# mLSTM decay rows loaded a step ahead, gate columns and sample squares moved, latent-stage weights in tiles of their own

## The chip, the cores and the metric

The kernel runs on one core of a Trainium2 chip. A core has TensorE (PE: matrix products and transposes; its weight loads are shown as PEld), VectorE (DVE), ScalarE (ACT), GpSimd (POOL) and SyncE (SP). Each engine works off its own instructions in order. A DMA is started by an instruction in the queue of SP, ACT or POOL, and then runs beside the engines. The metric is the time of one execution in device microseconds, and the median of several executions is compared.

## The reference

One inference step of a two-layer decoder trunk with a width of 1024. It works on 1024 new tokens of one sequence (the prompt) and on one new token for each of 8 running sequences (the samples), all in float32. The samples carry an mLSTM state in the first layer and 8192 cached positions, in pages of 128, in the second.

```python
# layer 0: x += mlstm(rmsnorm(x)); x += swiglu(rmsnorm(x))
q, k, v, o, gates = split(x @ w_in)         # 8 heads, 64 wide for q and k, 128 for v
i_pre = gates[:8];  log_f = log_sigmoid(gates[8:])
# chunk by chunk, per head; b is the running sum of log_f, m_t a running maximum
w_inter = exp(b + m - m_t)
w_intra = exp(b_t - b_s + i_s - m_t)        # for s <= t
s   = (q k^T) * w_intra
num = w_inter * (q C) + s v
den = w_inter * (q n) + sum(s)
h   = num / max(|den|, exp(-m_t))
C   = w_C * C + (w_s k)^T v;  n = w_C * n + sum(w_s k)
out = (rmsnorm_per_head(h) * g_head * sigmoid(o)) @ w_out

# layer 1: x += mla(rmsnorm(x)); x += swiglu(rmsnorm(x)); final rmsnorm
cq, ckv, k_rope = split(x @ w_in)           # 384, 256, 64 columns
q = rmsnorm(cq) @ w_uq                      # 8 heads, 128 plain + 64 rotary columns each
k_nope, v = rmsnorm(ckv) @ w_uk, rmsnorm(ckv) @ w_uv
out = softmax(q k^T * scale, causal) v @ w_o    # samples: over the cached pages as well
```

The outputs are the new activations, the new mLSTM states and the new latent and rotary key rows.

## The kernel before

**Products.** A product of two float32 matrices is made of three products in a faster format, since each factor is split in a high and a low part: `mm3` (L133 to L136) issues high x high, high x low and low x high into one PSUM bank. `split` makes the parts: ACT rounds a tensor to its high part (L117, or L120 with a scale per row), DVE or POOL subtracts it from the tensor for the low part (L118, L121). Activations lie transposed, features on the 128 partitions and tokens along the free axis, in chunks of 344 columns (1024 prompt and 8 sample tokens). A weight tile has 1024 rows and 128 columns. `load_w` loads one on SP's queue into one of two "wr" buffers and splits it into one of two pairs of "wh" and "wl" buffers; `linear` takes its products with all token chunks and hands each bank to an evacuation function.

**Order.** The order on each engine is not written out by hand. A scheduler of the tile framework places the instructions when the kernel is built, with the order of the program as priority, a cost model of its own, and the buffers: a tile asked for beyond its count of `bufs` waits until an older one of the same tag is released. Moving a call in the program therefore moves it in the priorities of all engines.

**mLSTM.** After the normalised input, the q and k tiles, the gates and the eight v tiles are computed (`mlstm`). `narrow` (L444) projects the 16 gate columns. `gates` (L534 to L590) turns them into running sums and maxima on 8 partitions and writes two sets of rows to memory: G_d, from which the decay between two tokens follows, and wi_d, the weights of the old state. It ends with eight transposes (L589), two groups of four, copied into `tok` (L590), which holds the per-token columns: a_t, w_s and exp(-m_t).

The loop at L485 then runs 16 steps, step i for chunk i//2 of 128 tokens and for half i%2 of the heads. A step is `mlstm_chunk`. It asks for Gb, a DMA of four rows of G_d spread over all 128 partitions (L600), and wb, two DMAs of rows of wi_d (L601 to L604), all on ACT's queue. From Gb, a_t and the causal mask DVE makes the exponent (L609, once per head), ACT its exponential (L610), and DVE multiplies it with the scores (L617). kt is k transposed and weighted by w_s (L623), vn is v transposed (L629) with a column of ones, qw is q times wb, on POOL (L634). PE forms the outputs from vn with Gb and from the state with qw (L642, L644), and the state's increment (L654); DVE updates the state C (L660), with the last column of wb as its factor; dn, the normalisation and its reciprocal square root follow on DVE (L202, L203 and L668 to L680). The step stops there (`yield`) and is finished a step later: the normalised output is transposed back and copied into v (L683, L684).

Between the first part of a step and the end of the step before stands other work of PE. For steps 1 to 8 it is `proj_o(i - 1)`, one tile of the output gate: its banks are read by DVE (L462) into `ot`, put through a tanh by ACT (L463) and stored to o_d. For steps 9 to 14 it is a tile of the output projection. `mlstm_sample` (L686 to L800) is a generator for the samples' states: it is advanced by one a step, twice in step 3, up to step 8. Each piece loads the state of one sequence (s_C), updates it on DVE (L781) and takes its products; the last piece takes the remaining products, s_h and its squares, and on PE the sum of the squares over the partitions (L796). In step 8 the input's buffers are released, o_d is loaded back (L473) and the first half of the tokens is gated (L478).

**Latent stage.** `mla` (from L1265) projects the kv latents (two tiles, `ev_k`), the 64 rotary key columns (`narrow`, `ev_r`) and three tiles of query latents (`ev_q`). The weights w_uk and w_uv, as two halves each, are needed later in split form in memory (uw_d). `up(i, f)` (L1339 to L1351) does one half: it loads it into a "wr" buffer on SP, for w_uk also transposes it, splits it into the pair "wh" and "wl" and stores both on POOL's queue. up(0, 0) and up(0, 1) follow the first two query tiles, up(1, 0) and up(1, 1) the third (L1353 to L1360).

`queries` (from L1425) makes each head's query. wq (L1432 to L1434) holds all of w_uq, three loads of 768 KB on POOL's queue. `rotary(0)` (L1455) and `plain(0)` (L1486) load their own columns of the first heads; the other heads split theirs out of wq. Queries are stored to qn_d and qr_d, and attention loads them back, for the first head on ACT's queue (L1585, L1587).

**Attention.** It mixes the prompt's heads with units of the samples' pages. The change touches four small DVE operations on one value per partition: the sum of two partial sums (L1679, 32 of them), the running maximum (L1829, 16), the running sum (L1836, 16) and its final scaling (L1863, 8). In the page loop DVE transposes the gathered rows (L1815) for PE (L1822).

The rest of the kernel, both feed-forward layers among it, is not touched.

## Time and profile before

| | us |
|---|---|
| median of 3 executions | 2671.79 |
| lowest and highest | 2664.44 and 2671.98 |
| the profiled execution | 2671.14 |
| span of the profiled execution | 2669.1 |
| gates and v tiles, about | 117 to 232 |
| the 16 mLSTM steps, about | 232 to 475 |
| output projection and first feed-forward layer, about | 475 to 1215 |
| latent projections, about | 1216 to 1305 |
| latent queries, about | 1305 to 1380 |
| attention, about | 1380 to 1885 |
| output projection, second feed-forward layer, end | 1885 to 2669 |

The profile shows one execution. The span runs from its first to its last instruction, and the rest of the time lies around it. Times of a row are us from the start of the span. In a row of the timeline stand the start, the duration, the engine, the line in the kernel, the operation, the tile written and the tiles read, their shapes, how many instructions of the kind stand in a row, and in brackets how long the engine had been idle before and what ended that. A tile's name is that of the program, but `wh`, `zh`, `ss`, `sc` and `mm` are used at many places. An idle engine costs time only if it is on the path that sets the end.

### The profile page before, as it was taken

Reading aid. Unit: us, or ns where it says so; the run is one execution under the profiler, and the core shown is the slowest. Engines: PE = TensorE matmul, PEld = TensorE weight load, DVE = VectorE, ACT = ScalarE, POOL = GpSimd, SP = SyncE. Lnnn points to the kernel's source line nnn. Section 1 sums busy time; section 2 is a strip of 40 time slices with the busy share of each in tenths; the row PEclk is TensorE's granted clock in tenths of the full one; section 3 lists DMA queues with packets and bytes.
Section 4 is the critical chain, followed back from the end, with each engine's and each line's share of the span. In section 5 each row is a group of like instructions: output and inputs, shape, how many; then the busy total and the mean of one; then the engine's idle time right before and its main releaser. Section 6 shows DMA issues by size and latency. Waiting matters only on the chain.

```text
span 2669.1 us, 54244 instructions
## 1 busy us (share of the span) xinstructions
PE 2523.4 (95%) x21151; PEld 2382.9 (89%) x21151; DVE 1865.6 (70%) x4491; ACT 1326.3 (50%) x3281; POOL 571.0 (21%) x574
## 2 busy tenths in 40 slices
PE   8999988999999999999888888889999999999998
PEld 8998886999999999999876666667899999999998
DVE  4345668898777777566557786667498877777755
ACT  4122234556555666453344555546355666555543
POOL 1000102201111111122334445442220111111102
PEclk9999989999999999999888999989999999999999
DMA  5133446526666656553666676554634756665653
GB/s 191 40 71 84 127 130 137 157 72 132 129 125 131 118 116 131 116 161 106 223 225 231 230 251 218 203 202 167 201 104 100 139 112 124 127 134 117 121 126 115
DMA packets 342519, 383.36 MB, mean 144 GB/s; under 512 B 23434, under 2 KB 274703, under 8 KB 333943
## 3 DMA queue, kind: packets, MB, share of 16 engines
q0 software_dynamic: 58880, 181.24, 29.2%
q1 hardware_dynamic: 258982, 182.30, 22.8%
q10 hardware_dynamic: 24400, 16.36, 2.6%
q8 instruction: 166, 2.72, 0.4%
q14 instruction: 91, 0.74, 0.1%
HBM read 254.12 MB, written 125.70 MB: 142 GB/s over the span
## 4 chain that ended last, share of the span: by engine, by line
PE 70%; DVE 13%; DMA 8%; ACT 4%; issue 3%; POOL 1%; SPq 1%; another core or an unknown queue 0%; POOLq 0%; ACTq 0%; DVEq 0%
PE sc L134 13%; PE sc L136 13%; PE sc L135 13%; PE mm L134 5%; PE mm L136 5%; PE mm L135 5%; DVE tt L1815 3%; PE ss L1847 2%; PE ss L134 2%; PE ss L136 2%; PE ss L135 2%; DMA Gb<-G_d 2%; PE ss L1822 2%; DVE wl L118 1%; PE mm L1718 1%
## 5 line engine op out<-in xcount | busy, mean ns | idle before, releaser
L1159 POOL DMA_DIRECT2D x_d<-wl x72 | 86.8, 1205 | 1003.1 <-DVE wl L1158 348.8
L117 ACT ACTIVATE wh<-wr 128x512 fp32r<-128x512 f32 (+2 forms) x169 | 136.6, 809 | 193.4 <-PE mm L135 125.1
L1815 DVE STREAM_TRANSPOSE tt<-nat 128x1024 f32<-128x1024 f32 x128 | 154.1, 1223 | 10.7 <-PE ss L1822 6.7
L118 DVE TENSOR_TENSOR wl<-wr,wh 128x1024 fp32r<-128x1024 f32 (+2 forms) x82 | 98.4, 1200 | 37.2 <-ACT wh L117 28.5
L134 PE MATMUL mm<-zh,wh 128*128 128x344 f32 x320 | 104.7, 327 | 8.0 <-DVE ot L462 8.0
L1822 PE MATMUL ss<-tt,qbd 128*32 128x128 f32 x2560 | 94.6, 283 | 16.1 <-DVE tt L1815 10.8
L118 DVE TENSOR_TENSOR b<-u,b 128x256 fp32r<-128x256 f32 (+1 forms) x252 | 103.2, 423 | 9.2 <-ACT b L117 7.9
L117 ACT ACTIVATE b<-u 128x256 fp32r<-128x256 f32 (+1 forms) x252 | 98.8, 414 | 15.8 <-PE ss L136 6.3
L1159 POOL DMA_DIRECT2D x_d<-st x72 | 105.1, 1459 | 4.2 <-DVE dC L118 4.2
L118 DVE TENSOR_TENSOR wh<-S,wh 128x512 fp32r<-128x512 f32 x108 | 74.6, 690 | 42.5 <-ACT wh L117 42.5
L135 PE MATMUL mm<-zl,wh 128*128 128x344 f32 x320 | 103.8, 324 | 0.0
L136 PE MATMUL mm<-zh,wl 128*128 128x344 f32 x320 | 103.6, 324 | 0.0
L1822 PEld LDWEIGHTS ss<-tt,qbd 128*32 128x32 f32 x2560 | 73.0, 113 | 33.7 <-DVE tt L1815 20.1
L117 ACT ACTIVATE wh<-S 128x512 fp32r<-128x512 f32 x108 | 67.9, 629 | 59.5 <-PE sc L136 39.8
L1718 PE MATMUL mm<-wh,vt 128*128 128x256 f32 (+1 forms) x320 | 76.7, 301 | 10.6 <-ACT wh L117 5.5
L134 PE MATMUL sc<-zh,wh 128*128 128x344 f32 x256 | 83.0, 325 | 1.0 <-ACT wh L117 0.8
L136 PE MATMUL sc<-zh,wl 128*128 128x344 f32 x256 | 82.1, 321 | 0.7 <-DVE wl L118 0.7
L135 PE MATMUL sc<-zl,wh 128*128 128x344 f32 x256 | 82.1, 321 | 0.0
L1718 PEld LDWEIGHTS mm<-wh,vt 128*128 128x128 f32 x320 | 56.9, 199 | 22.0 <-ACT wh L117 9.2
L1677 ACT ACTIVATE wr<-sc,mx,rqt 128x512 f32<-128x512 f32 (+2 forms) x96 | 64.1, 673 | 20.7 <-DVE mx L1672 10.8
L1808 POOL DMA_INDIRECT nrp<-in_cache_k_rope_dram,idx x64 | 61.8, 966 | 56.3 <-DVE tt L1815 21.7
L1807 POOL DMA_INDIRECT nat<-in_cache_latent_dram,idx x64 | 61.1, 954 | 57.2 <-PE ss L1847 43.6
(1075 smaller groups left out, 10678.0 us busy)
## 6 DMA issues: line engine op xcount, KB each, us to landing
wr<-in_ffn_w_gate_up_dram SPq DMA_DIRECT2D x96, 512.0 KB
x_d<-st POOLq DMA_DIRECT2D x72, 520.0 KB
x_d<-wl POOLq DMA_DIRECT2D x72, 512.0 KB
dr<-in_ffn_w_down_dram SPq DMA_DIRECT2D x72, 256.0 KB
wr<-in_mlstm_w_in_dram SPq DMA_DIRECT2D x24, 512.0 KB
wr<-in_mlstm_w_out_dram SPq DMA_DIRECT2D x16, 512.0 KB
q<-qn_d SPq DMA_DIRECT2D x28, 256.0 KB
wr<-in_mla_w_o_dram SPq DMA_DIRECT2D x14, 512.0 KB
```

The costliest lines, as they stand in the source:

```text
L117: ins = nc.scalar.activation(hi, src, AF.Copy)
L118: self.low = e.tensor_tensor(lo, src, hi.bitcast(F32), op=ALU.subtract)
L134: mm(ps, wh, xh, start=start, stop=False, **kw)
L135: mm(ps, wh, xl, start=False, stop=False, **kw)
L136: self.last = mm(ps, wl, xh, start=False, stop=stop, **kw)
L1159: nc.gpsimd.dma_start(self.x_d[:, 2 * dp:2 * dp + 2, 512 * i:512 * i + 2 * PW[i]], st[i], accum_op=ALU.add)
L1677: nc.scalar.activation(px[:, ks], o, AF.Exp, bias=mx[:, 0:1], scale=f, accum_out=sm[:, c:c + 1])
L1718: nc.tensor.matmul(o, x, y, start=i == 0, stop=i == len(ops) - 1)
L1807: nc.gpsimd.indirect_dma_start(out=nat[:, s].rearrange("p s c -> p (s c)"), out_offset=None, in_=lat, in_offset=ix)
L1808: nc.gpsimd.indirect_dma_start(out=nrp[:, s].rearrange("p s c -> p (s c)"), out_offset=None, in_=rop, in_offset=ix)
L1815: V.transpose(out=tt, in_=src.rearrange("p s (c i) -> p c s i", i=32))
L1822: nc.tensor.matmul(psS[32 * j:32 * j + 32, u * P:u * P + P], self.qbd[:, b, cb], tt[:, c, 4 * j:4 * j + 4].rearrange("p s k -> p (s k)"), ...
```

## The change

Six edits. (1) `gates` no longer makes the transposes into `tok`; it returns them as a function, `turned`, which is called after the fifth v tile. (2) The loads of Gb and wb move out of `mlstm_chunk` into `decay`. The loop calls it for the first step ahead of the loop and then in each step for the next one. Gb has four buffers instead of three, wb three as before, qw one instead of two. The factor of the state update, which was read from wb, is copied to a small tile wc by POOL first. (3) The sample generator has one more `yield`, ahead of the sum of squares, and step 8 advances it once more, ahead of the last output-gate tile. (4) `up` writes its parts to tiles uh and ul of a pool of its own. up(1, 0) stands after the second kv tile and up(1, 1) after the rotary key columns. (5) wq holds five heads (3 to 7), 480 KB a load; the plain columns of heads 1 and 2 come by two loads on ACT's queue into a "wr" tile, `pair`; four tiles of the rotary step are asked for ahead of wq. (6) The four small operations of attention become tensor-scalar forms, in which a per-partition operand takes the place of one or two of the tensors.

```diff
@@ mlstm
-        self.gates(p1, pg, gi, lf, bcol)
+        turned = self.gates(p1, pg, gi, lf, bcol)
...
         for j in range(8):
             proj_v(j)
+            if j == 4:
+                turned()
...
+        due = [self.decay(pi, 0, 0)]
         for i in range(16):
-            g = self.mlstm_chunk(pi, i // 2, i % 2, q, k, v)
+            if i < 15:
+                due.append(self.decay(pi, (i + 1) // 2, (i + 1) % 2))
+            g = self.mlstm_chunk(pi, i // 2, i % 2, q, k, v, *due.pop(0))
             next(g)
+            if i == 8:
+                next(smp, None)
             if 1 <= i <= 8:
                 proj_o(i - 1)
...
@@ gates
-        for hf in range(2):
-            ps = self.tp()
-            ...
+        def turned():
+            for hf in range(2):
+                ps = self.tp()
+                for j in range(4):
+                    c = hf * 4 + j
+                    nc.tensor.transpose(ps[:, j * 96:(j + 1) * 96], p3[:, c * L:(c + 1) * L], self.ident[:96, :96])
+                V.tensor_copy(self.tok[:, hf * 4:hf * 4 + 4], ps[:, :384].rearrange("p (j i r) -> p j i r", j=4, i=3)[:, :, :, 0:8])
+        return turned
...
+    def decay(self, pi, c, hg):
+        nc = self.nc
+        s = slice(c * L, (c + 1) * L)
+        Gb = self.t(pi, [P, 4, L], "Gb", bufs=4)
+        nc.scalar.dma_start(Gb, self.G_d[hg * 4:hg * 4 + 4, s].unsqueeze(0).to_broadcast([P, 4, L]))
+        wb = self.t(pi, [P, 2, L], "wb", bufs=3)
+        for hh in range(2):
+            src = self.wi_d.rearrange("(hp hh) s -> hh hp s", hh=2)[hh, hg * 2:hg * 2 + 2, s]
+            nc.scalar.dma_start(wb[hh * 64:(hh + 1) * 64], src.unsqueeze(0).to_broadcast([64, 2, L]))
+        return Gb, wb
...
@@ mlstm_chunk
-            qw = self.t(pi, [P, 2, L], "qw", bufs=2)
+            qw = self.t(pi, [P, 2, L], "qw", bufs=1)
             nc.gpsimd.tensor_tensor(qw, q[:, j2, s], wb, op=ALU.mult)
+            wc = self.t(pi, [P, 2], "wc", bufs=3)
+            nc.gpsimd.tensor_copy(wc, wb[:, :, L - 1])
...
-                V.scalar_tensor_tensor(C[r, h], C[r, h], wb[r, h // 2, L - 1:L], ps[r, h // 2], op0=ALU.mult, op1=ALU.add)
+                V.scalar_tensor_tensor(C[r, h], C[r, h], wc[r, h // 2:h // 2 + 1], ps[r, h // 2], op0=ALU.mult, op1=ALU.add)
@@ mlstm_sample
         V.tensor_tensor(h2, hs, hs, op=ALU.mult)
+        yield
         ps = self.tp()
         nc.tensor.matmul(ps[:, 0:64], self.ones, h2, start=True, stop=True)
@@ mla
+        upp = self.pool("up")
...
-            wh, wl = (self.t(self.wp, [P, KT * P], x, F32R) for x in ("wh", "wl"))
+            wh, wl = (self.t(upp, [P, KT * P], x, F32R) for x in ("uh", "ul"))
...
         self.linear(lw(QL + P, P), z, KT, P, ev_k(1))
+        up(1, 0)
         self.page_index(mt)
...
         self.narrow(wr, 64, 64, z, "wh", ev_r)
+        up(1, 1)
...
-        for f in range(2):
-            up(1, f)
@@ queries
+        self.rf = [[self.t(qs, [P, CW], "rf" + i, bufs=2) for i in "ab"] for _ in range(2)]
-        wq = self.t(qs, [P, 3, 8, 192], "wq")
+        wq = self.t(qs, [P, 3, 5, 192], "wq")
         for k in range(3):
-            nc.gpsimd.dma_start(wq[:, k].rearrange("p h c -> p (h c)"), wuq[k * P:(k + 1) * P, :])
+            nc.gpsimd.dma_start(wq[:, k].rearrange("p h c -> p (h c)"), wuq[k * P:(k + 1) * P, 576:])
...
-            raw = wq[:, :, h, 0:P]
             if h == 0:
...
+                pair = self.t(self.wp, [P, KT * P], "wr")[:, : 6 * P].rearrange("p (k h m) -> p k h m", h=2, m=P)
+                for i in range(2):
+                    nc.scalar.dma_start(pair[:, :, i], self.wsrc(wuq, 0, 3, 192 * (i + 1), P))
+                first.append(pair)
+            else:
+                raw = first[0][:, :, h - 1] if h < 3 else wq[:, :, h - 3, 0:P]
@@ attention
-                    V.tensor_tensor(sm[:, 0:1], sm[:, 0:1], sm[:, 1:2], op=ALU.add)
+                    V.tensor_scalar(sm[:, 0:1], sm[:, 0:1], sm[:, 1:2], None, op0=ALU.add)
...
-        V.scalar_tensor_tensor(nb, rm, -SCALE, self.nb, op0=ALU.mult, op1=ALU.min)
+        V.tensor_scalar(nb, rm, -SCALE, self.nb, op0=ALU.mult, op1=ALU.min)
...
-        V.scalar_tensor_tensor(self.lrow, self.lrow, al, ls, op0=ALU.mult, op1=ALU.add)
+        V.tensor_scalar(self.lrow, self.lrow, al, ls, op0=ALU.mult, op1=ALU.add)
...
-            V.tensor_tensor(self.lrow, self.lrow, fac, op=ALU.mult)
+            V.tensor_scalar(self.lrow, self.lrow, fac, None, op0=ALU.mult)
```

More of the change, by code (lines that the diff above doesn't have):

```diff
@@ L513, in mlstm @@
                     gated(*loaded(ob()[:, :256], 1, h, first))
-        tiles = [self.t(pi, [P, 4, L], "Gb", bufs=3).rearrange("p h t -> p (h t)")] + [ob() for _ in range(3)]
+        tiles = [self.t(pi, [P, 4, L], "Gb", bufs=4).rearrange("p h t -> p (h t)")] + [ob() for _ in range(3)]
         tiles += [self.t(pi, [P, 4, 129], "vn", bufs=3).rearrange("p h t -> p (h t)") for _ in range(2)] + [ob() for _ in range(2)]
@@ L584, in gates, with mlstm_chunk @@
         self.tok = self.t(p1, [P, NCK, 3, 8], "tok")
-        for hf in range(2):
-            ps = self.tp()
-            for j in range(4):
-                c = hf * 4 + j
-                nc.tensor.transpose(ps[:, j * 96:(j + 1) * 96], p3[:, c * L:(c + 1) * L], self.ident[:96, :96])
-            V.tensor_copy(self.tok[:, hf * 4:hf * 4 + 4], ps[:, :384].rearrange("p (j i r) -> p j i r", j=4, i=3)[:, :, :, 0:8])
-    def mlstm_chunk(self, pi, c, hg, q, k, v):
+        def turned():
[16 more added lines that the diff above has]
+        return Gb, wb
+    def mlstm_chunk(self, pi, c, hg, q, k, v, Gb, wb):
         nc = self.nc
@@ L598, in mlstm_chunk @@
         j2 = slice(hg * 2, hg * 2 + 2)
-        Gb = self.t(pi, [P, 4, L], "Gb", bufs=3)
-        nc.scalar.dma_start(Gb, self.G_d[h4, s].unsqueeze(0).to_broadcast([P, 4, L]))
-        wb = self.t(pi, [P, 2, L], "wb", bufs=3)
-        for hh in range(2):
-            src = self.wi_d.rearrange("(hp hh) s -> hh hp s", hh=2)[hh, j2, s]
-            nc.scalar.dma_start(wb[hh * 64:(hh + 1) * 64], src.unsqueeze(0).to_broadcast([64, 2, L]))
         a_t, ws_t, em_t = (self.tok[:, c, r, h4] for r in range(3))
@@ L1351, in up @@
                 nc.gpsimd.dma_start(self.uw_d[i, k, :, f], x.bitcast(F32))
+        lw = lambda c0, m: self.load_w(self.wsrc(w_in, 0, KT, c0, m), KT, m)
+        for a in self.lead:
+            ev_k(0)(*a)
+        self.linear(lw(QL + P, P), z, KT, P, ev_k(1))
+        up(1, 0)
+        self.page_index(mt)
+        wr = self.t(self.wp, [P, KT * P], "wr")[:, :KT * 64].rearrange("p (k m) -> p k m", m=64)
+        nc.sync.dma_start(wr, self.wsrc(w_in, 0, KT, QL + KVL, 64))
+        self.narrow(wr, 64, 64, z, "wh", ev_r)
+        up(1, 1)
+        self.rs_of(s2, KVL)
+        for c in range(NCH):
+            cs = slice(c * CW, (c + 1) * CW)
+            w = slice(c * CW, min((c + 1) * CW, S))
+            for j in range(2):
+                V.scalar_tensor_tensor(kf[:, j, cs], kf[:, j, cs], self.gcol(self.G_KV + j), s2[:, cs], op0=ALU.mult, op1=ALU.mult)
+                self.split(ckh[:, j, w], ckl[:, j, w], kf[:, j, w], lo_eng=nc.gpsimd)
         for j in range(3):
@@ L1398, in mla @@
         mt.release()
+        upp.release()
         self.rsp.release()
@@ L1455, in rotary @@
         def rotary(h0):
-            raw = wq[:, :, h0:h0 + 4, P:]
+            raw = wq[:, :, 1:, P:]
             if h0 == 0:
@@ L1473, in chunk @@
                 for e, (x, y) in enumerate(((rc, rn), (rn, rc))):
-                    f, g = (self.t(qs, [P, CW], "rf" + i, bufs=2) for i in "ab")
+                    f, g = self.rf.pop(0) if self.rf else (self.t(qs, [P, CW], "rf" + i, bufs=2) for i in "ab")
                     V.tensor_tensor(f, ps[0], x[:, cs], op=ALU.mult)
@@ L1502, in plain @@
             return chunk
-        stores = []
+        stores, first = [], []
         for op in ORDER.split():
```

15 lines of the change are left out of this document (removed).

## The prediction

> **What bounds the kernel now.** I read the page first, then busy times by stage, then the waits of TensorE (PE) and VectorE (DVE) in the stages that the change touches, and last the timelines around each wait. The page's span, busy line and chain of waits:
>
> ```profile
> span 2669.1 us, 54244 instructions
> ...
> PE 2523.4 (95%) x21151; PEld 2382.9 (89%) x21151; DVE 1865.6 (70%) x4491; ACT 1326.3 (50%) x3281; POOL 571.0 (21%) x574
> ...
> PE 70%; DVE 13%; DMA 8%; ACT 4%; issue 3%; POOL 1%; SPq 1%; another core or an unknown queue 0%; POOLq 0%; ACTq 0%; DVEq 0%
> ```
>
> PE is busy 95% of the span, and 70% of the chain is PE. No matrix product goes away in this change, so the most that can be won is PE's idle time, 2669.1 - 2523.4 = 145.7 us, and PE's time at a low clock, and only where the change acts. By stage (window, length, busy time of PE, PEld, DVE, ACT, POOL, PE's granted clock, DMA share, GB/s): mLSTM steps with the output gate, the later steps, latent projections (two rows), latent queries, the middle of attention.
>
> ```profile
> 245.00:410.00 165.00, 150.40 (x993) 138.66 (x994) 106.44 (x343) 54.53 (x159) 15.37 (x25) 0.93 0.48 135
> 410.00:475.00 65.00, 56.27 (x340) 44.88 (x339) 55.05 (x191) 27.64 (x86) 16.86 (x19) 0.97 0.54 109
> 1215.00:1256.00 41.00, 39.53 (x259) 37.01 (x257) 26.93 (x67) 13.72 (x27) 4.70 (x6) 1.00 0.22 78
> 1256.00:1305.00 49.00, 46.57 (x294) 43.84 (x293) 24.48 (x48) 22.42 (x43) 25.04 (x32) 0.93 0.52 166
> 1305.00:1380.00 75.00, 68.38 (x404) 64.30 (x402) 47.28 (x137) 32.70 (x75) 17.26 (x27) 0.89 0.66 232
> 1500.00:1700.00 200.00, 170.92 (x2183) 136.37 (x2187) 148.06 (x319) 106.90 (x280) 98.79 (x97) 0.99 0.68 231
> ```
>
> PE idles 14.6, 8.7, 1.5, 2.4, 6.6 and 29.1 us in these. All of what follows fits inside these numbers, the gates' 4.55 us and the clocks of 0.89 and 0.93.
>
> **Gate columns (turned).** PE, in order, came to the eight transposes of L589 before their rows were ready:
>
> ```profile
> 152.83 0.88 PE L589 MATMUL ss<-ct,p 96*128 96x96 f32 x8 [3.04 <-ACT p L577]
> ...
> 172.78 0.63 ACT L610 ACTIVATE Gb<-Gb 128x512 f32<-128x512 f32 x1 [6.62 <-DVE Gb L609]
> ...
> 174.41 0.43 PE L134 MATMUL sc<-zh,wh 128*128 128x344 f32 x1 [0.83 <-ACT wh L117]
> 175.67 0.42 PE L136 MATMUL sc<-zh,wl 128*128 128x344 f32 x1 [0.68 <-DVE wl L118]
> ```
>
> The 0.88 us of transposes are the same work wherever they stand. Placed after the fifth v tile, they wait for rows that were complete some 30 us before, and v products stand where the 3.04 us wait was. The second group has the same cure by another way: ScalarE (ACT) stood 6.62 us at L610, an exponential of the first step's decay that had been drawn forward into the v products, and the v weights' split L117 was queued behind it. The decay needs tok, and tok now comes later, so L610 cannot stand there. 3.04 + 0.83 + 0.68 = 4.55 us; I take 4, since the v tile that moves up may be short of its own weights by a fraction. Ends 1 and 4.55.
>
> **Decay rows a step ahead.** Waits (engine, line, cause: us in all, times, longest): DVE at 245 to 475, DVE at 410 to 475, and PE at 117 to 460.
>
> ```profile
> DVE Gb L609 <- DMA Gb<-G_d: 27.5, 9, 5.4
> DVE s_C L781 <- DMA s_C<-in_state_mlstm_C_dram: 10.1, 5, 6.0
> ...
> DVE Gb L609 <- DMA Gb<-G_d: 5.2, 3, 2.3
> ...
> PE mm L134 <- DVE ot L462: 8.0, 6, 2.4
> PE ss L796 <- DVE s_h L794: 1.2, 1, 1.2
> PE ss L654 <- DVE sfu L202: 2.4, 1, 2.4
> ```
>
> DVE's 27.5 us are not the price: an idle DVE costs only where PE comes to wait. How it does is seen in one step, and a second one looks alike but is not:
>
> ```profile
> 310.06 1.14 DVE L609 SCALAR_TENSOR_TENSOR Gb<-Gb,tok,ct 128x128 f32<-128x128 f32 x4 [4.05 <-DMA Gb<-G_d]
> 314.77 0.52 DVE L462 TENSOR_TENSOR ot<-mm,rs 128x344 f32<-128x344 f32 x1
> 315.35 0.55 PE L134 MATMUL mm<-zh,wh 128*128 128x344 f32 x1 [2.36 <-DVE ot L462]
> ...
> 290.71 0.69 DVE L781 TENSOR_TENSOR s_C<-s_C,s_wsb 128x512 f32<-128x512 f32 x1 [6.04 <-DMA s_C<-in_state_mlstm_C_dram]
> 296.01 0.42 PE L134 MATMUL mm<-zh,wh 128*128 128x344 f32 x1 [2.30 <-DVE ot L462]
> ```
>
> DVE waits for the decay rows, its queue holds the eviction L462 of an output-gate product, and PE waits for that bank. At 296 the late one is the sample state's load s_C, which the change does not touch. So 8.0 - 2.30 = 5.7 us hang on Gb. With four buffers and the load traced one step ahead, a step of about 20 us (eight in the 165 us above) lies between issue and use. s_C then becomes the late one, in the steps where it is late already. I take 4 of 5.7 (ends 0 and 5.7) and 1 us for the clock, which is 0.93 over this stage (ends 0 and 2).
>
> After 410 us DVE is busy 55.05 of 65 us: it sets the pace, so its 5.2 us of Gb waits could count in full, but behind them stand its other partners (PE, ACT). I take 2, ends 0 and 5.2.
>
> Issues: the three triggers a step are those of before, on the same ACT queue, so no issue time is added; the first step's three are joined by the second's before the loop, where ACT is idle over half of the time. The new copy wc is 14 POOL instructions, at most 0.73 us by the nearest larger one,
>
> ```profile
> 268.02 0.73 POOL L634 TENSOR_TENSOR qw<-q,wb 128x256 f32<-128x256 f32 x1 [15.02 <-PE sc L644]
> ```
>
> and POOL is busy 15.4 of 165 us here; the state update L660 that reads wc waits for PE's L654 anyway. Nothing; uncovered, 14 x 0.73 = 10 us of POOL. One qw buffer instead of two is paid by the same 15.02 us of POOL's idle time.
>
> **Sample squares.** In the ninth step PE waits 1.2 us at L796 for s_h. With the split it goes on with gate products. But the output of that step then waits for its o_d reload, and the 2.4 us at L654 sit behind the gating that this feeds, so what is won early is partly waited for there. I take 0.5, ends 0 and 1.2.
>
> **Latent projections and queries.** PE's waits at 1215 to 1380, then the rows at the places:
>
> ```profile
> PE sc L134 <- ACT wh L117: 7.1, 3, 4.0
> PE sc L136 <- DVE wl L118: 1.6, 4, 0.7
> ...
> 1216.33 0.63 ACT L117 ACTIVATE wh<-wr 128x512 fp32r<-128x512 f32 x1 [8.23 <-PE mm L135]
> 1245.00:1255.00 10.00, 8.55 (x53) 8.11 (x51) 9.81 (x22) 4.47 (x9) 0.57 (x1) 1.00 0.10 39
> 1252.72 1.06 ACT L117 ACTIVATE wh<-wr 128x1024 fp32r<-128x1024 f32 x1 [1.06 <-DVE wl L118]
> 1317.77 0.42 PE L134 MATMUL sc<-cqh,wh 128*128 128x344 f32 x1 [3.99 <-ACT wh L117]
> 1317.19 0.94 ACT L117 ACTIVATE wh<-wq 128x384 fp32r<-128x384 f32 x2 [3.67 <-DMA qr_d<-qx]
> 1316.64 0.37 ACTq L1585 DMA_DIRECT2D q<-qn_d  x1
> 1315.00:1325.00 10.00, 6.50 (x25) 6.06 (x26) 5.50 (x20) 2.59 (x6) 2.16 (x4) 0.70 0.77 256
> 1325.00:1335.00 10.00, 10.00 (x63) 10.00 (x62) 5.17 (x13) 5.08 (x12) 0.00 (x0) 0.96 0.71 253
> ```
>
> Of 7.1 us, 3.99 belong to the queries, the other 3.1 to the projections; of 1.6, I give half to each. The projections' 3.1 + 0.8 = 3.9 us come from weight splits that stand late in a DVE busy 9.81 of 10 us, while the second halves wh, wl of the up-projection hold the pair of weight buffers. Two of the four up-projection splits (1.06 us each on ACT) now come earlier, the first of them able to use the 8.23 us in which ACT waits, and none uses the pair any more. I take 3, ends 0 and 3.9.
>
> In the queries the split of the second head's weights (L117) ran at 1317.19, when 3 x 768 KB of wq had landed; PE waited 3.99 us and did 25 products in the 10 us window, where the next has 63. Now heads 1 and 2 come by two loads of 192 KB of their own and wq has 5/8 of its bytes. 3.99 + 0.73 = 4.7 us of waits; the clock of 0.70: 25 products took 6.50 us, 0.26 each against 10/63 = 0.16, 2.5 us too long. I take 4 + 1.5 = 5.5, ends 0 and 7.2. Against it stands that ACT's queue held a load of q (L1585) right before the split, which needs a store to land.
>
> **Four tiny operations in attention.** Per line: shortest, median, longest in ns.
>
> ```profile
> L1829 DVE SCALAR_TENSOR_TENSOR nb<-rm,nb x16: 110/153/3506, 1413.8 to 1839.6; 128x1 f32<-128x1 f32 x16
> L1679 DVE TENSOR_TENSOR sm<-sm x32: 111/152/1606, 1399.5 to 1873.2; 128x1 f32<-128x1 f32 x32
> L1672 DVE TENSOR_SCALAR mx<-mx,rqt x32: 229/265/275, 1385.8 to 1870.6; 128x1 f32<-128x1 f32 x32
> ...
> PE ss L1822 <- DVE tt L1815: 10.8, 12, 2.6
> ```
>
> The forms that read two tensors take up to 1.6 and 3.5 us; L1672, a tensor-scalar form of the same shape with two pointers, never exceeds 275 ns in 32, though POOL is as busy beside it (98.79 of 200 us). One 2.61 us wait of PE at L1822 follows the 3.506 us one. The change costs 72 x (265 - 153) = 8 us of DVE at most, spread over 500 us of attention, where it is busy 74% (148.06 of 200), and takes away the few long ones. I take 2; ends -3 (what of the 8 us falls in the places where PE waits for DVE) and +9 (the two maxima and as much again).
>
> [...]
>
> **Sum.** 4 + 4 + 1 + 2 + 0.5 + 3 + 5.5 + 2 = 22 us. The profiled execution took 2671.14 us, 2.04 outside its span; less 22 is 2649.1. The median of the runs is 2671.79, 0.65 higher, so 2650. All upper ends together are 4.55 + 5.7 + 2 + 5.2 + 1.2 + 3.9 + 7.2 + 9 = 38.8, giving 2633; at the lower ends 1 us is won at the gates and 3 lost in attention, giving 2674.
>
> **Rivals.** *Waits only move.* s_C stays late on DVE (10.1 us) in the steps where Gb was, DVE sets the pace after 410, and the ACT queue's load L1585 keeps the query split where it is. Only gates 4, projections 3 and 2 of attention are left: 2663. For it: L1585 stands 0.55 us ahead of the split, and a 6.04 us s_C wait produced the same PE wait as Gb. Against: a wait of 5 us on Gb was alone in most steps.
>
> *It does not come earlier.* The loads are traced earlier, but ACT is in order and its queue is as long; if the instruction order keeps the triggers behind the step before, as now, 4 + 1 + 2 of the steps are lost: 2657.
>
> [...]
>
> *Slower: triggers that block ACT.* A decay load that needs a buffer not yet free holds ACT's whole queue: vn copies, tanh of the gates, exponentials. The row at 172.78 shows ACT held 6.62 us by such a step and PE paying 1.5 right behind. Were every one of 15 steps to cost PE the largest wait seen, 2.36 us, that is 35 us more, with 4 + 3 + 5.5 + 2 = 14.5 won elsewhere: 2692. It decides from 14.5/15, about 1 us a step. Against: Gb has four buffers for two steps in use, and wc frees wb early.
>
> **How the numbers follow.** The forecast has 0.53, moved waits 0.17, no earlier loads 0.13, shared port 0.09, blocked ACT 0.08. No change, for this kernel, is within 0.3%, 8 us of 2671.8. Forecast, no earlier loads and shared port are faster, less a tenth of the forecast's share that may fall short, plus half of the moved waits: 0.78. Same 0.13, slower 0.09. The range reaches from the upper ends, 2634, past the moved waits to 2666.
>
> **What would show it.** Right: no TensorE wait at the transposes, Gb waits on DVE under 5 us in all, TensorE's wait for ot near 2.3, no 1.45 us wait at the second query tile, clock above 0.9 at 1315, no tiny operation above 0.4 us. Wrong: L609 still waits for its load, an exponential or copy on ACT stands behind a trigger, or waits of 3 us appear at the projections.

## The result, and the profile after

The changed kernel took 2656.17 us (median of 6 runs, 2644.99 to 2657.70), the kernel before 2669.31 us (median of 6, 2664.44 to 2671.98). The ratio is 0.9944, with a 95% interval from 0.9926 to 0.9961: 13 to 15 us faster, where 22 were forecast. A second group of runs, on another chip, gave 0.9950 (0.9933 to 0.9968).

The profiled execution took 2652.47 us. The page of the changed kernel, as shown of before:

```profile
span 2650.7 us, 54288 instructions
...
PE 2520.7 (95%) x21151; PEld 2377.0 (90%) x21151; DVE 1861.4 (70%) x4491; ACT 1326.0 (50%) x3281; POOL 570.8 (22%) x588
...
PE 73%; DVE 11%; DMA 7%; ACT 5%; issue 3%; POOL 1%; SPq 0%; another core or an unknown queue 0%; ACTq 0%; POOLq 0%; DVEq 0%
```

PE's idle time fell from 145.7 to 2650.7 - 2520.7 = 130.0 us, and its busy time by 2.7 us. To see where, I divided each trace at the same instructions: the first transposes of v in step 0 (L628 before, L644 after), the last eviction of the output gate (L462, L464), the last transposes back of a step (L683, L701), the last product of the norm before the latent stage (L253), the last transposes after the query tiles (L1366, L1385), the first score (L1660, L1686) and the last product of attention (L1718, L1744). Each mark is the start of its row in the timeline. The lengths between these marks, in us; the changed kernel was profiled three times in all (two of these are among the experiments below):

| stretch | before | changed, three profiles | difference |
|---|---|---|---|
| start to the first step | 221.8 | 220.9, 220.3, 219.6 | -0.9 to -2.2 |
| steps with the output gate | 151.2 | 150.6, 149.4, 152.7 | -1.9 to +1.4 |
| later steps | 101.3 | 96.5, 97.8, 97.5 | -3.5 to -4.8 |
| output projection and feed-forward | 743.7 | 742.1, 742.4, 743.6 | -0.1 to -1.6 |
| latent projections | 67.6 | 64.2, 63.4, 64.0 | -3.4 to -4.2 |
| latent queries | 74.6 | 67.1, 67.0, 67.2 | -7.3 to -7.5 |
| attention | 523.8 | 523.7, 520.9, 524.1 | -2.9 to +0.3 |

Three more kernels below (with the up-projection halves, w_uq or the small operations as before the change) have the changed kernel's order of instructions on PE, DVE and ACT up to the end of the steps, so they show how far these rows scatter: their first steps began at 221.8, 222.9 and 219.9 us, and their later steps took 99.3, 97.2 and 97.0 us. So the first row shows no gain beyond its scatter. The gain lies in the latent stage, some 11 us, and in the later steps, some 2 to 5. The gates and the steps with the output gate, for which 9 us were forecast, gave nothing beyond theirs. Why is seen first in the waits of the changed kernel, DVE at 232 to 475 us and PE at 117 to 232 and 232 to 460:

```profile
DVE Gb L625 <- DMA Gb<-G_d: 26.2, 8, 6.2
...
PE sc L134 <- ACT wh L117: 2.7, 1, 2.7
...
PE mm L134 <- DVE ot L464: 6.5, 5, 2.0
PE sc L660 <- DVE Gb L633: 5.5, 3, 3.7
```

DVE still waits 26.2 us for the decay rows, where it was 27.5. The wait at the gate transposes (3.0 us) is gone, and a wait of 2.7 us stands at a weight split. The timelines of the changed kernel, DVE and ACT around the end of the v tiles, and PE:

```profile
187.27 1.12 DVE L625 SCALAR_TENSOR_TENSOR Gb<-Gb,tok,ct 128x128 f32<-128x128 f32 x4
193.43 1.14 DVE L625 SCALAR_TENSOR_TENSOR Gb<-Gb,tok,ct 128x128 f32<-128x128 f32 x4 [3.01 <-DMA Gb<-G_d]
199.09 1.64 DVE L625 SCALAR_TENSOR_TENSOR Gb<-Gb,tok,ct 128x128 f32<-128x128 f32 x4 [4.33 <-DMA Gb<-G_d]
...
203.03 1.14 DVE L625 SCALAR_TENSOR_TENSOR Gb<-Gb,tok,ct 128x128 f32<-128x128 f32 x4 [1.87 <-DMA Gb<-G_d]
...
204.21 0.63 ACT L626 ACTIVATE Gb<-Gb 128x512 f32<-128x512 f32 x1 [2.80 <-DVE Gb L625]
204.90 2.01 ACT L117 ACTIVATE wh<-wr 128x1024 fp32r<-128x1024 f32 x2
...
206.01 0.43 PE L134 MATMUL sc<-zh,wh 128*128 128x344 f32 x1 [2.71 <-ACT wh L117]
207.27 0.42 PE L136 MATMUL sc<-zh,wl 128*128 128x344 f32 x1 [0.68 <-DVE wl L118]
```

As soon as tok exists, the scheduler puts the exponents (L625) and exponentials (L626) of as many steps as there are Gb buffers ahead of all else: four groups now. The kernel before had three, the last exponential at 172.78. DVE and ACT wait for one load after the other, and the weight split L117 stands behind the fourth exponential. In the loop it goes on in the same way. ACT's queue, then DVE and PE, in two steps of the changed kernel:

```profile
244.17 0.40 ACTq L608 DMA_DIRECT2D Gb<-G_d  x1
252.47 1.14 DVE L625 SCALAR_TENSOR_TENSOR Gb<-Gb,tok,ct 128x128 f32<-128x128 f32 x4 [6.21 <-DMA Gb<-G_d]
...
309.38 1.14 DVE L625 SCALAR_TENSOR_TENSOR Gb<-Gb,tok,ct 128x128 f32<-128x128 f32 x4 [3.74 <-DMA Gb<-G_d]
310.44 0.16 DVE L687 TENSOR_TENSOR dn<-dn,tok 128x4 f32<-128x4 f32 x1
...
314.80 0.43 PE L134 MATMUL mm<-zh,wh 128*128 128x344 f32 x1 [2.02 <-DVE ot L464]
```

After four groups ahead of the loop, the load at 244.17 is that of the fifth step: it is a step earlier than before. But the exponents that read it are a step earlier too, and DVE comes to them 2.1 us after the issue and waits 6.21 us for the rest of the load. The rows of dn and ot that PE needs stand behind them, as before the change. A second theory was that the load itself is late, because its trigger stands on ACT behind the copy of the step before.

The latent stage came out as worked out. Busy times of the changed kernel by stretch (columns as in the prediction):

```profile
1216.00:1280.00 64.00, 62.47 (x390) 58.18 (x389) 39.28 (x71) 28.89 (x60) 22.74 (x24) 1.00 0.34 110
1300.00:1341.00 41.00, 40.63 (x254) 39.56 (x253) 34.86 (x102) 17.36 (x40) 11.48 (x18) 1.00 0.80 277
```

PE idles 1.5 us in the projections and 0.4 us in these 41 us of the queries, and its clock is 1.00 in both. Over the whole stretch of the queries, as marked in the table, the clock was 0.91 before and is 0.97 now.

### The profile page after: what moved, and what is told of

It reads as the page before. It is cut to its first block, busy times and chain, and to the rows that moved or that the text cites. A ratio compares the mean times of both kernels' runs of the same rounds, so it can differ in the third digit from the quotient of the medians.

```text
span 2650.7 us, 54288 instructions
## 1 busy us (share of the span) xinstructions
PE 2520.7 (95%) x21151; PEld 2377.0 (90%) x21151; DVE 1861.4 (70%) x4491; ACT 1326.0 (50%) x3281; POOL 570.8 (22%) x588
## 4 chain that ended last, share of the span: by engine, by line
PE 73%; DVE 11%; DMA 7%; ACT 5%; issue 3%; POOL 1%; SPq 0%; another core or an unknown queue 0%; ACTq 0%; POOLq 0%; DVEq 0%
PE sc L134 13%; PE sc L136 13%; PE sc L135 13%; PE mm L134 6%; PE mm L136 5%; PE mm L135 5%; PE ss L1873 2%; PE ss L134 2%; PE ss L136 2%; PE ss L135 2%; DVE tt L1841 2%; DMA Gb<-G_d 2%; PE ss L1848 2%; DVE wl L118 1%; PE mm L1744 1%
## 5 line engine op out<-in xcount | busy, mean ns | idle before, releaser
L117 ACT ACTIVATE wh<-wr 128x512 fp32r<-128x512 f32 (+2 forms) x167 | 133.4, 800 | 179.9 <-PE mm L135 111.0
L1841 DVE STREAM_TRANSPOSE tt<-nat 128x1024 f32<-128x1024 f32 x128 | 153.9, 1223 | 16.7 <-PE ss L1848 13.0
L118 DVE TENSOR_TENSOR wl<-wr,wh 128x1024 fp32r<-128x1024 f32 (+2 forms) x80 | 93.0, 1164 | 27.1 <-ACT wh L117 26.4
L117 ACT ACTIVATE b<-u 128x256 fp32r<-128x256 f32 (+1 forms) x252 | 99.0, 415 | 15.8 <-PE ss L136 6.3
L1848 PE MATMUL ss<-tt,qbd 128*32 128x128 f32 x2560 | 94.0, 280 | 11.8 <-issue 6.3
L118 DVE TENSOR_TENSOR wh<-S,wh 128x512 fp32r<-128x512 f32 x108 | 74.6, 691 | 42.9 <-ACT wh L117 42.8
L1848 PEld LDWEIGHTS ss<-tt,qbd 128*32 128x32 f32 x2560 | 72.2, 112 | 29.5 <-issue 12.9
L117 ACT ACTIVATE wh<-S 128x512 fp32r<-128x512 f32 x108 | 68.0, 630 | 59.6 <-PE sc L136 39.7
L1744 PE MATMUL mm<-wh,vt 128*128 128x256 f32 (+1 forms) x320 | 79.4, 309 | 10.0 <-ACT wh L117 5.6
L1873 PE MATMUL ss<-nat,pz 128*32 128x256 f32 x1024 | 68.6, 401 | 11.2 <-ACT pz L1869 10.6
L1703 ACT ACTIVATE wr<-sc,mx,rqt 128x512 f32<-128x512 f32 (+2 forms) x96 | 64.2, 674 | 26.8 <-DVE mx L1698 13.1
L1744 PEld LDWEIGHTS mm<-wh,vt 128*128 128x128 f32 x320 | 58.0, 205 | 21.7 <-ACT wh L117 9.7
```

Source lines behind the costliest of these rows:

```text
L117: ins = nc.scalar.activation(hi, src, AF.Copy)
L118: self.low = e.tensor_tensor(lo, src, hi.bitcast(F32), op=ALU.subtract)
L1703: nc.scalar.activation(px[:, ks], o, AF.Exp, bias=mx[:, 0:1], scale=f, accum_out=sm[:, c:c + 1])
L1744: nc.tensor.matmul(o, x, y, start=i == 0, stop=i == len(ops) - 1)
L1841: V.transpose(out=tt, in_=src.rearrange("p s (c i) -> p c s i", i=32))
L1848: nc.tensor.matmul(psS[32 * j:32 * j + 32, u * P:u * P + P], self.qbd[:, b, cb], tt[:, c, 4 * j:4 * j + 4].rearrange("p s k -> p (s k)"), ...
```

## The experiments

All kernels below are the changed kernel with the edit shown. They ran in three groups, each on a chip of its own; times are compared within a group only. In the first group the kernel before took 2642.87 us, in the second 2669.83 us, in the third 2671.15 us (median of 16). In the first two groups every kernel ran once. The changed kernel's own six runs lie up to 13 us apart, so a single time says little, and the lengths of the stages decide.

**The decay rows in their own step again.** Three buffers for Gb, two for qw, the state's factor read from wb.

```diff
-        due = [self.decay(pi, 0, 0)]
...
-            if i < 15:
-                due.append(self.decay(pi, (i + 1) // 2, (i + 1) % 2))
-            g = self.mlstm_chunk(pi, i // 2, i % 2, q, k, v, *due.pop(0))
+            g = self.mlstm_chunk(pi, i // 2, i % 2, q, k, v, *self.decay(pi, i // 2, i % 2))
...
-        Gb = self.t(pi, [P, 4, L], "Gb", bufs=4)
+        Gb = self.t(pi, [P, 4, L], "Gb", bufs=3)
```

> The changed kernel, with the decay rows loaded in their own step again, into three buffers, qw in two and the state factor read from wb; all else as changed. Theory A (the order on VectorE): with a buffer more, the load and the exponents that read it both stand one step earlier, so the wait for the load is the same. It expects VectorE's waits for Gb between 24 and 29 us as in both kernels, TensorE's waits for ot between 5 and 8 us, and the end of the 16 steps within 1.5 us of the changed kernel's 474. Theory B (the extra buffer does shorten what TensorE waits for, and something else ate it): TensorE's waits in the steps up to 460 us grow by 4 us or more, and the steps end 4 us or more later.

The 474 us in this text is the end in the kernel before; the changed kernel's is 468.11. Measured: 2636.30 us against 2642.87 before, steps' end 465.29, which is 2.8 us earlier and outside the 1.5 us of theory A; the steps began earlier by more than that, as is told below. DVE's waits at 232 to 480, PE's, and ACT at the v tiles:

```profile
DVE Gb L622 <- DMA Gb<-G_d: 27.3, 9, 5.0
...
PE mm L134 <- DVE ot L464: 6.1, 5, 2.6
...
199.56 0.63 ACT L623 ACTIVATE Gb<-Gb 128x512 f32<-128x512 f32 x1 [3.42 <-DVE Gb L622]
...
200.91 1.06 ACT L117 ACTIVATE wh<-wr 128x1024 fp32r<-128x1024 f32 x1 [0.71 <-PE sc L136]
```

The waits are what theory A gave, and theory B's longer waits did not come: the load ahead with its fourth buffer wins nothing in the steps (248.9 us from the first step to the end of the steps, against 247.2 to 250.2 with it). It even seems to cost ahead of them. With three buffers the last exponential is over at 200.2, the split waits for PE and not PE for the split, and the first step begins at 216.4 us, 3 to 4.5 us before the changed kernel's three profiles. The chip is another one here, so this number is shown once only; the order of the rows is shown.

**The exponents behind the normalised outputs of the step before.**

```diff
-        for h in range(4):
-            V.scalar_tensor_tensor(E[:, h], Gb[:, h], a_t[:, h:h + 1], ...)
+        with self.tc.issue_after(self.hn.ins) if hasattr(self, "hn") else nullcontext():
+            for h in range(4):
+                V.scalar_tensor_tensor(E[:, h], Gb[:, h], a_t[:, h:h + 1], ...)
```

> The changed kernel, with the exponents of a step (the four VectorE operations that read Gb first) placed behind the normalised outputs of the step before on VectorE. The loads stay as they are. Theory A: the loads have landed by then, VectorE's waits for Gb fall from 26 to under 8 us, TensorE's waits for ot from 6.5 to under 3 us, and the 16 steps end 3 us or more earlier than in the changed kernel. Theory B (the load is late whatever stands first): the waits for Gb stay above 15 us. A third outcome: the waits go, but the scores' product now waits for the later exponents, and the steps end no earlier.

2630.04 us against 2642.87. No wait of DVE for a decay load is left in the steps, which refutes theory B: the load is early enough as soon as something else stands first. PE's waits at 232 to 480 us:

```profile
PE ss L702 <- DVE Gb L698: 5.3, 5, 1.8
PE mm L134 <- ACT zh1h L120: 4.5, 1, 4.5
...
PE mm L134 <- DVE ot L464: 0.7, 1, 0.7
```

PE's wait for ot fell from 6.5 to 0.7 us as theory A gave, but the outputs (L698) are now late and the later steps grew to 103.6 us. The steps took 247.7 us, no less than in the changed kernel: the third outcome. The first step began at 216.4 us, since only one step's exponents now stand in the v tiles.

**The exponents behind the state update only.** The same edit, but after the last operation of L678 in place of the normalised outputs.

```diff
+                self.cu = V.scalar_tensor_tensor(C[r, h], C[r, h], wc[r, h // 2:h // 2 + 1], ps[r, h // 2], ...)
...
+        with self.tc.issue_after(self.cu.ins) if hasattr(self, "cu") else nullcontext():
```

> The changed kernel, with the exponents of a step placed only behind the state update of the step before on VectorE, some 3 to 5 us earlier in the queue than behind its normalised outputs. Theory A: waits for Gb under 12 us, and the steps end 2 us or more earlier than in the changed kernel; the exponents are less late for the scores than with the stronger hold. Theory B: waits above 15 us.

2629.47 us against 2642.87. No Gb wait on DVE, and the steps took 145.2 + 97.7 = 242.9 us, 4 to 7 less than in the changed kernel's three profiles and 6 less than in the first experiment, on the same chip. Theory A stands.

**The gate columns turned after the eighth v tile.**

```diff
-            if j == 4:
+            if j == 7:
                 turned()
```

> The changed kernel, with the gate columns turned after the eighth v tile instead of the fifth. Theory A: the 2.71 us wait at 206 us is the first decay rows again, which follow tok on VectorE and ACT and hold up a weight split; with no v tile left behind tok it goes, and the first step begins about 2.7 to 3.4 us earlier than 220.9 us, unless the first step then waits for its own decay rows, which take 7 to 8 us from issue: then a wait of up to 8 us stands in the first step in its place. Rival: the wait belongs to a late weight load, and stays at the same tile.

2644.06 us against 2642.87: no gain is left. The v tiles run through, the first step begins at 215.4 us, and then the price comes in it. PE's timeline of this kernel:

```profile
222.12 1.13 PE L672 MATMUL ss<-vn,kt 128*64 128x129 f32 x8 [3.30 <-issue]
227.48 2.09 PE L660 MATMUL sc<-vn,Gb 128*128 128x129 f32 x8 [2.79 <-DVE Gb L633]
```

The wait at 206 us was thus that of the decay work, and not of a weight load. But then the first step waits, 3.30 and 2.79 us in the rows above, and the steps with the output gate took 163.3 us here, 11 to 14 us more.

**The changed kernel once more.** No edit.

> The changed kernel as it is, once more, so that the other three have it beside them on the same chip. The 2.71 us wait of TensorE at the weight split near 206 us and VectorE's waits for Gb of 24 to 29 us come again, and the 16 steps end some 247 us after the first step's transposes of v, as in its first trace (220.93 to 468.11).

2648.39 us against 2669.83. The wait at the split was 2.0 us, those for Gb 25.1, the steps took 247.2 us.

**The up-projection halves as before.**

```diff
-        upp = self.pool("up")
-            wh, wl = (self.t(upp, [P, KT * P], x, F32R) for x in ("uh", "ul"))
+            wh, wl = (self.t(self.wp, [P, KT * P], x, F32R) for x in ("wh", "wl"))
...
-        up(1, 0)
-        up(1, 1)
...
+        for f in range(2):
+            up(1, f)
```

> The changed kernel with the up-projection halves split into the wh and wl buffers again, and both halves of w_uv after the third query tile. If the projections' gain comes from this edit, the stretch from the end of the norm before the projections to the last transposes of the query tiles takes 3.4 us more than in the changed kernel (67.6 against 64.2 us in the first two traces), with waits of 1.4 and 1.7 us at the query tiles' weights. Rival: the gain came with the shift of everything before it, and the stretch stays at 64 us.

2673.02 us against 2669.83. PE's waits from the start of the latent stage to the first score:

```profile
PE sc L136 <- DVE wl L118: 3.7, 4, 1.9
PE sc L134 <- ACT wh L117: 3.1, 2, 1.7
```

The projections took 68.5 us, 5.1 more than in the changed kernel beside it (63.4): the gain is this edit's. The queries behind them also took 4.3 us more (71.3 against 67.0), at a clock of 0.94 against 0.97, though their own edit was in place. The two edits are thus not separate to the last us. That the steps, long before this edit, also ended 7.8 us later than beside it is not explained by it; L464's waits were 9.8 us here and 5.5 there. Equal steps thus differ by several us from one execution to the next, and the whole difference of the two times is not the edit's.

**All of w_uq in one tile.** The fifth edit undone as a whole, the rotary tiles asked for ahead of wq included.

```diff
-        wq = self.t(qs, [P, 3, 5, 192], "wq")
+        wq = self.t(qs, [P, 3, 8, 192], "wq")
...
-            nc.gpsimd.dma_start(..., wuq[k * P:(k + 1) * P, 576:])
+            nc.gpsimd.dma_start(..., wuq[k * P:(k + 1) * P, :])
...
-                pair = ...
```

> The changed kernel with all of w_uq in one tile again, loaded in three pieces of 768 KB, and heads 1 and 2 split out of it. If the load's size and place held the second head, the stretch from the query tiles' last transposes to the first score takes 7.4 us more than in the changed kernel (74.6 against 67.1), with a wait of about 4 us before the second head's products. Rival (the ACT queue's load of q held the split): half of that or less.

2658.13 us against 2669.83, and 2648.39 for the changed kernel. PE's timeline:

```profile
1307.40 0.65 PE L134 MATMUL sc<-cqh,wh 128*128 128x344 f32 x1 [3.60 <-ACT wh L117]
```

The queries took 72.5 us, 5.4 more than beside it (67.0), and the wait is back at the second head, so the edit is what won it. By the expectation's own measure this speaks for the load. The traces say otherwise. ACT's rows in this kernel, and then in the changed one:

```profile
1306.27 0.37 ACTq L1605 DMA_DIRECT2D q<-qn_d  x1
1306.82 0.94 ACT L117 ACTIVATE wh<-wq 128x384 fp32r<-128x384 f32 x2 [3.45 <-DMA qr_d<-qx]
...
1300.53 0.53 ACT L117 ACTIVATE wh<-wr 128x384 fp32r<-128x384 f32 x1 [0.95 <-PE mm L135]
...
1303.13 0.38 ACTq L1611 DMA_DIRECT2D q<-qn_d  x1
```

The last of the 384 packets of wq (6144 bytes each) ended at 1301.4 us in this trace, 5 us ahead of the split. (The bracket names a store of qr_d, which the split does not read.) What stands right ahead of the split in ACT's queue is the trigger of the load of q, and that went off when the store of q had landed (1306.25). It is the same in the kernel before: the last packet of wq ended at 1311.9, the trigger L1585 went off at 1316.64, and the split ran at 1317.19. With weights in a tile of their own the scheduler places the split ahead of the trigger. So ACT's queue held the split, as the rival has it, and the edit took the wait away by the order of that queue; this experiment alone could not tell the two apart, since it puts the split back behind the trigger. Whether the smaller load adds something of its own, by letting the store land earlier, is not shown.

**Order without the load ahead.** The edits of the first and the third experiment together: the exponents behind the state update, the decay rows loaded in their own step into three buffers.

> The exponents placed behind the state update of the step before on VectorE, as in the earlier kernel with that placement, but with the decay rows loaded in their own step into three buffers, qw in two and the factor read from wb. If the order alone decides, the 16 steps take as long as with the load a step ahead, about 243 us from the first step's transposes of v to the last step's end, 4 us or more less than in the changed kernel, and VectorE's waits for Gb stay under 5 us. If the earlier load is needed as well, the waits for Gb are 10 us or more and the steps take about as long as in the changed kernel.

2638.87 us against 2669.83 before and 2648.39 for the changed kernel. DVE's waits at 232 to 480:

```profile
DVE ot L464 <- PE mm L136: 16.0, 8, 3.3
...
DVE Gb L623 <- DMA Gb<-G_d: 3.0, 3, 1.3
```

Of the Gb waits 3.0 us are left. The first step began at 215.2 us and the steps took 235.9 us, 11 less than in the changed kernel. The order decides; the load ahead is not needed.

**Three kernels timed.** The changed kernel, the one just told of, and the changed kernel with the four small operations in their old forms:

```diff
-                    V.tensor_scalar(sm[:, 0:1], sm[:, 0:1], sm[:, 1:2], None, op0=ALU.add)
+                    V.tensor_tensor(sm[:, 0:1], sm[:, 0:1], sm[:, 1:2], op=ALU.add)
-        V.tensor_scalar(nb, rm, -SCALE, self.nb, op0=ALU.mult, op1=ALU.min)
+        V.scalar_tensor_tensor(nb, rm, -SCALE, self.nb, op0=ALU.mult, op1=ALU.min)
```

(L1862 and L1889 in the same way.)

> The changed kernel once more, timed beside the other kernels of this group on the same chip: 0.990 to 0.997 of the kernel before.

2658.57 us (8 runs, 2652.37 to 2662.02), ratio 0.9950 (0.9933 to 0.9968).

> The kernel with the exponents behind the state update and the decay rows loaded in their own step into three buffers, timed. Its steps ended 16 us earlier than the changed kernel's. If what is won there is kept to the end, its time is 8 to 16 us below that of the changed kernel, 0.985 to 0.992 of the kernel before. If the later stages give it back (attention takes another order), it is within 4 us of the changed kernel.

2643.14 us (6 runs, 2638.83 to 2652.70), ratio 0.9897 (0.9872 to 0.9921). What the order wins is kept to the end: 15 us below the changed kernel, and 28 below the kernel before. The steps took 236.6 us in its profile.

> The changed kernel with the four small attention operations in their old forms with two tensors. If these forms are stretched beside work of GpSimd, some of the 72 take over 0.8 us again, 5 to 10 us of VectorE in all, and the time is 1 to 4 us above that of the changed kernel. If the stretching is hidden, or the new forms cost as much elsewhere, the times agree within 1 us. [...]

2658.72 us (9 runs, 2653.76 to 2662.86), ratio 0.9953 (0.9936 to 0.9969): the same as with the new forms. Of the old forms, in this kernel:

```profile
L1855 DVE SCALAR_TENSOR_TENSOR nb<-rm,nb x16: 112/150/3494, 1395.3 to 1829.7; 128x1 f32<-128x1 f32 x16
L1705 DVE TENSOR_TENSOR sm<-sm x32: 111/150/1620, 1379.2 to 1863.3; 128x1 f32<-128x1 f32 x32
```

And of the new ones, in the changed kernel:

```profile
L1855 DVE TENSOR_SCALAR nb<-rm,nb x16: 172/208/216, 1400.8 to 1817.9; 128x1 f32<-128x1 f32 x16
L1705 DVE TENSOR_SCALAR sm<-sm x32: 171/204/216, 1383.7 to 1854.6; 128x1 f32<-128x1 f32 x32
```

The stretching goes with the form: up to 3494 and 1620 ns on these two lines in the old form, at most 216 ns in the new. Each of the nine old-form instructions over 0.5 us ran beside a tensor-tensor operation of POOL, the one of 3.494 us beside three of about 1.28 us each. In the kernel before, 14 of the 72 ran beside such an operation, the longest for 3.51 us, and the others took at most 0.22 us; in the changed kernel's first profile it was 7 of 72, the longest of them 0.23 us. All 72 together took 21.1 us of DVE in the old forms and 15.3 in the new, though the median of the new is some 50 ns longer. PE's waits for the transposed rows (L1841) and for ACT's pz, at 1370 to 1830 us, with the old forms and then in the changed kernel:

```profile
PE ss L1848 <- DVE tt L1841: 10.5, 11, 2.6
...
PE ss L1873 <- ACT pz L1869: 6.8, 9, 1.6
...
PE ss L1873 <- ACT pz L1869: 10.6, 9, 3.8
...
PE ss L1848 <- DVE tt L1841: 3.5, 7, 1.2
```

So 7 us of waits behind the transposes go with the edit, in all three profiles of the changed kernel (3.3 to 3.5 us), and the waits for pz grow in part of their place (7.7 to 11.8 us). In the time nothing of it can be told with 8 and 9 runs: each interval reaches some 4.5 us to either side, so a gain of 2 us is neither shown nor excluded. The profile of the old forms had a longer attention (534.8 us against 524.1); as the next kernel, with the new forms, also has 533.6 there, the length of the stage alone is no sign of the edit.

**The sample's last piece whole.**

```diff
         V.tensor_tensor(h2, hs, hs, op=ALU.mult)
-        yield
...
-            if i == 8:
-                next(smp, None)
             if 1 <= i <= 8:
```

> The changed kernel with the last piece of the sample's generator whole again, in its old place. In the changed kernel TensorE waits 0.7, 3.4 to 3.7 and 2.4 to 2.8 us around the end of the output gate; the kernel before waits 1.2, 0.8, 2.4 and 0.7 there. If the split only moved the wait, the 3.5 us wait for the scores' product goes, a wait of 1 to 2 us at the sum of squares comes, and from the last gate eviction to the end of the steps it takes no more time than in the changed kernel. If the split helps, that stretch grows by 0.5 us or more.

One run, 2668.11 us. PE's timeline after the last gate tile, in the changed kernel:

```profile
374.71 0.49 PE L660 MATMUL sc<-vn,Gb 128*128 128x129 f32 x2 [0.68 <-ACT vn L645]
380.22 0.80 PE L660 MATMUL sc<-vn,Gb 128*128 128x129 f32 x2 [3.71 <-DVE Gb L633]
385.81 1.13 PE L672 MATMUL ss<-vn,kt 128*64 128x129 f32 x8 [2.36 <-DVE v L819]
```

and in the kernel with the piece whole:

```profile
374.13 0.66 PE L812 MATMUL ss<-s_h,ones 128*128 128x64 f32 x2 [1.23 <-DVE s_h L810]
376.89 0.80 PE L658 MATMUL sc<-vn,Gb 128*128 128x129 f32 x2 [0.68 <-ACT vn L643]
385.67 1.13 PE L670 MATMUL ss<-vn,kt 128*64 128x129 f32 x8 [2.37 <-DVE sfu L202]
388.52 0.69 PE L636 MATMUL ss<-ct,k 128*128 128x128 f32 x2 [0.68 <-ACT v L700]
```

In step 8 itself the split only moved the wait: 0.68 + 3.71 + 2.36 = 6.8 us now, 1.23 + 0.68 + 2.37 + 0.68 = 5.0 us without it, and L672 comes 14.24 us after the last gate eviction with the split and 14.61 us without. Yet from that eviction to the end of the steps it is 101.7 us without, as in the kernel before (101.3), and 96.5 to 97.8 us with the split. The stretch behind L672 makes the difference, as busy times of 14 and 16 us from the last eviction show, first with the split:

```profile
371.57:385.57 14.00, 7.29 (x44) 5.79 (x42) 9.84 (x26) 3.94 (x14) 0.72 (x1) 0.77 0.84 233
385.57:401.57 16.00, 15.76 (x86) 12.95 (x87) 14.56 (x45) 9.67 (x23) 1.26 (x5) 0.89 0.63 190
```

and then without it:

```profile
371.06:385.06 14.00, 10.34 (x52) 8.49 (x50) 9.71 (x25) 3.93 (x14) 0.73 (x1) 0.61 0.88 245
385.06:401.06 16.00, 14.71 (x70) 11.72 (x71) 13.15 (x39) 8.62 (x20) 1.11 (x4) 0.70 0.43 122
```

In the second 16 us PE gets 86 products done in place of 70, at a granted clock of 0.89 in place of 0.70. In the five other profiles with the changed kernel's order the same two stretches were granted 0.74 to 0.82 and then 0.80 to 0.89, and in the kernel before, without the split, 0.64 and then 0.78. The later steps took 96.5 to 99.3 us in the six profiles with the split and 101.3 and 101.7 us in the two without. So the split goes with 2 to 5 us there, and not where it acts. Over all 16 steps it cannot be told: 249.9 us without it, 246.6 to 253.4 us in the six with it.

## Why the prediction was right or wrong

The time, 2656, lies 6 us above the forecast of 2650 and in its range; the gain was 13 to 15 us instead of 22. That it is this near is in part luck: the gates, the decay rows and the small operations, 13 of the 22 us, gave nothing that can be shown, and the latent stage and the later steps gave more than their terms. The terms:

- **Gates, 4 forecast, nothing measurable.** The first step began at 219.6 to 222.9 us in six profiles with this order, and at 221.8 before. The wait at L589 went as described. The step that failed is "L610 cannot stand there": tok comes later, but it comes before the last three v tiles, and the exponentials were drawn forward to it again, four of them instead of three (the row at 172.78 is that of the third step, and not of the first as the prediction has it). 2.71 + 0.68 us of waits took the place of 0.83 + 0.68, and PE's clock fell to 0.92 and 0.91 in the 20 us from 200 us on (1.00 from 160 to 232 us before the change). Where fewer exponentials stood in the v tiles, the first step began 5 to 7 us earlier than before the change (215.2 to 216.4 against 221.8), so the term was of about the right size; with three exponentials and no fourth buffer it began at 216.4 us, in one profile, which points to the fourth buffer as what gave it back.
- **Decay rows, 4 + 1 + 2 forecast, 0 measured.** "A step of about 20 us lies between issue and use" failed. The load moved a step ahead and its first use moved along, to 2.1 us behind the issue, and DVE, in order, then waits 6 us. The scheduler places that use; by what reckoning is not shown. That DVE's queue order hands the wait on to ot and PE was right: with the order changed and nothing else, DVE's wait and PE's wait for ot both went (from 26.2 us to none and from 6.5 to 0.7 us with the exponents behind the normalised outputs). The rival "it does not come earlier" had the effect and the price right, and the reason wrong: the triggers do come earlier. That its 2657 is nearest to the measured time is chance, since the gates were lost as well and other terms gave more.
- **Sample squares, 0.5 forecast, 2 to 5 measured.** In step 8 the start of L672 moved by 0.4 us, near the number but not by the mechanism: PE's waits there grew from 5.0 to 6.8 us, and with them stands a higher clock (0.77 in place of 0.61). The rest came behind it, with a clock that is less low (0.89 in place of 0.70), and the term had left this out.
- **Projections, 3 forecast, 3.4 to 4.2 measured; queries, 5.5 forecast, 7.3 to 7.5 measured** (5.1 and 5.4 when each was undone alone). Waits and clock went where the prediction had them, and the queries' term was taken too low. But its reason for the queries was wrong: wq had landed 5 us before the split, and the size of its load was not what PE waited for. The split stood behind ACT's load of q, as the rival "waits only move" has it; that it would stay there was the rival's error. That the term came out is luck so far as it was worked out from the load.
- **Small operations, 2 forecast, nothing measurable in the time.** Stretching gone, as the row of L1672 let expect: the 72 of them stayed at or under 276 ns in three profiles of the changed kernel, where the old forms took up to 3.5 us beside POOL's tensor-tensor operations. The prediction's chances give 0.09 to a shared port, the case in which POOL stretches the new forms too; it did not come, and no run shows a port. The prediction feared 8 us more of DVE work, and it was 5.8 us less. PE's wait of 2.6 us behind the transposes went, as forecast; what the prediction left out is that other waits of the stage, for pz, grow where these go.
- **Blocked ACT**, the slower rival, did not come in the steps. What holds the weight split at 204 us, once, for 2.7 us of PE, is an exponential that waits for its rows, and not a trigger that waits for a buffer.

## What to carry to other kernels

An earlier load helps an in-order engine only if its first reader stays where it is: when a scheduler moves the reader along with the load, one more buffer moves the wait and does not shorten it (27.3 us on DVE with three buffers here, 24.0 to 26.6 with four). Look at what stands behind the waiting instruction in its queue, and pin the reader behind work that is ready; here that was worth 15 us more than the change, with one buffer less. A load or a column made ready early is also an invitation to draw work forward, so see what it will be put in front of. And before a wait is put down to a load's size, see in the trace when the load had landed: here the weights lay ready for 5 us, and what stood ahead in the queue was a trigger that waited for something else.

## What the runs showed of the hardware that was not expected

More waiting, spread in another way, went with a higher clock: 6.8 us of waits in step 8 with a granted clock of 0.77 and then 0.89, and 5.0 us of waits with 0.61 and then 0.70. The other profiles named with the last experiment fall on the same two sides. So the sum of the waits alone did not set the clock in these rows; what did is not shown.

One stage differs between the groups. On the chip of the first group, attention took 500 to 510 us in all four kernels, on the others 521 to 535 us in the changed kernel and its relatives, while the other stages agreed within their scatter. PE's waits at the page products that no other engine explains (L1848 "issue", 6.3 us in the changed kernel's first profile, 5.5 and 6.0 in the others) are not listed for any of the four on that chip. Whether the chip makes the difference is not shown, since none of the four ran on another one.
